# The modulation vector's sixty tiles: from pairs of loads inside the FFN to single loads spread from the merge to the FFN's end

## The chip, the cores and the metric

The kernel runs on one core of a Trainium2 chip. The core has five engines with a queue of instructions each: TensorE (PE, the matmuls, with its weight loads shown apart as PEld), VectorE (DVE), ScalarE (ACT), GpSimd (POOL) and SyncE (SP, which here only issues DMA transfers). Each engine works off its queue in order, and a wait at the head of a queue holds up all that stands behind it. The metric is the time of one execution on the device in microseconds (us); lower is better.

## The reference

Two layers follow each other on 512 tokens of width 1024, in fp32. The first is a hybrid of attention and a state space, with a gated FFN and a per-layer embedding (PLE). The second is a block whose norms and residuals are modulated by a vector computed from a conditioning vector `c_2`:

```python
# first layer, second half
h = h + (gate_attn * attn_d + gate_ssm * ssm_d) @ w_out          # merge, w_out
n2 = rmsnorm(h, g_ffn)
h = h + (silu(n2 @ w_ffn_gate) * (n2 @ w_ffn_up)) @ w_ffn_down   # FFN
h = h + sigmoid(h @ w_ple_gate) * (p_l @ w_ple_proj)             # PLE
...
# second layer
c_act = silu(c_2)
mod = c_act @ w_ada + b_ada                  # [6 * 1024], w_ada is 1024 x 6144
shift1, scale1, gate1, shift2, scale2, gate2 = split(mod, 6)
h = rmsnorm(x, norm1_g) * (1 + scale1) + shift1
proj = h @ w_in
...
```

`mod` depends on the inputs alone, so it can be computed anywhere before the second layer.

## The kernel before, in words

All activations lie feature-major, 128 features by 512 tokens to a tile. A product in fp32 is three matmuls: each operand is split into a high part and a rest (`wh`, `wl` for weights, `..h`, `..l` for activations), and `mm()` issues `wh` by high (L159), `wh` by rest (L160) and `wl` by high (L161). One matmul here has 128 x 128 weights and 512 tokens.

Weights come in tiles of 128 x 1024 fp32 (512 KB). `weights()` allocates a raw tile `wr` (three buffers), issues its load on SP's queue (L150), lets ACT copy the high part to `wh` (L122) and DVE subtract for `wl` (L123); `wh`/`wl` have two buffers. It does so at a priority 40 places ahead of the code around it. The next load into a `wr` buffer is issued when the `wl` that reads it has ended. The order on each engine is set by a scheduler, by priorities in the order of the program.

The stages that the change touches, all in `block_1` (their stretches in the profile in brackets): the gates (to 447.87 us); the **merge** (447.87 to 513.15), 8 turns of 36 matmuls with one `w_glu` tile each and one `w_ap` tile every second turn, after which DVE forms `gb` (L874) and `g` (L873, L875), POOL adds and DVE splits (L129); **w_out** (513.15 to 561.87), 8 turns of 24 matmuls; **gate/up** (561.87 to 813.87), 22 turns of 48 matmuls with one `w_fg` and one `w_fu` tile each; **down** (819.30 to 924.02 without its first stripe), 8 stripes of 66 matmuls with three weight tiles each. Then PLE and the second layer, whose first use of `mod` is at L950.

The modulation vector is the generator `modulation()` (L315). It broadcasts `c_2` over all partitions (L320) and applies Silu (L321) to get `ca`; then, for each of 48 tiles of `w_ada`, it loads 512 KB into `wa` (two buffers, L324) and runs one DVE multiply-and-reduce over 1024 elements (L325), which gives 128 entries of `mod`. Two further tables of 6 tiles each (`w_lat_t`, `w_up_t`) are reduced in the same way (L348, L349) against a row of `mod` that small matmuls (L343) and ACT (L345) broadcast. In all there are 60 loads and 60 reductions. Before, the generator is opened in stage gate/up and advanced twice at the end of each turn of it, and twice in each of the 8 iterations of down as long as anything is left:

```python
for f in range(22):
    ...
    hid.append(self.split_new(hp, f"hid{f}", a))
    for _ in range(2):
        next(mod, None)
```

Of the kernel before, what the change touches and what calls it, by code (L numbers as in the profile page):

```python
# [84 lines left out]
class Program:  # L85
# [53 lines left out]
    def weights(self, ap, n, eng=None, pool=None, bufs=1, parts=1):  # L139

        r = self.t(self.wp, "wr", (128, 8, 128), F32, 3)
        if pool is None:
            h, l = self.pair(self.wp, "w", (128, 8, 128), 2)
        else:
            h, l = self.pair(pool, "ws", (128, n, 128), bufs)
        p0 = self.tc.cur_priority
        self.tc.cur_priority = max(0, p0 - WLEAD[self.phase])
        for i in range(0, n, n // parts):
            b = slice(i, i + n // parts)
            self.Q.dma_start(r[:, b], ap[:, b])  # L150
            self.last_split = self.split(h[:, b], l[:, b], r[:, b], eng)
        self.tc.cur_priority = p0
        return h, l
# [161 lines left out]
    def modulation(self, pool):  # L315
# [6 lines left out]
        for n in range(48):  # L322
            w = self.t(pool, "wa", (128, 1024), bufs=2)
            self.Q.dma_start(w, self.d["w_ada"][n])  # L324
            V.tensor_tensor_reduce(out=w, in0=w, in1=ca, op0=OP.mult, op1=OP.add, scale=1.0, scalar=0.0,  # L325
                                   accum_out=self.mod[:, n:n + 1])
            if n % 8 == 7:
                m = self.mod[:, n - 7:n + 1]
                V.tensor_tensor(out=m, in0=m, in1=self.col("b_ada", n - 7, 8), op=OP.add)
                if n // 8 in (1, 4):  # L330
                    V.tensor_scalar(m, m, 1.0, None, op0=OP.add)
            yield
        self.eb = self.t(self.cp, "eb", (128, len(LAT) + 2 * UPS))
        n = 0
        for m, tab, c in ((0, "w_lat_t", len(LAT)), (3, "w_up_t", 2 * UPS)):
# [10 lines left out]
            for i in range(c):  # L346
                w = self.t(pool, "wa", (128, 1024), bufs=2)
                self.Q.dma_start(w, self.d[tab][i])  # L348
# [3 lines left out]
                yield  # L352

# [406 lines left out]
    def block_1(self):  # L760
# [89 lines left out]
        self.phase = 2  # L850
        m_cm, m = self.open("M")
# [8 lines left out]
        for j in range(8):  # L860
# [16 lines left out]
            self.split_half(merged[j][0], merged[j][1], ga)  # L877
        b_cm.__exit__(None, None, None)
# [8 lines left out]
        for j in range(8):  # L887
# [9 lines left out]
            self.add_square(wo, acc, self.res[j], j == 0)  # L897
        self.y = y
# [7 lines left out]
        mod = self.modulation(hp)  # L906
        hid = []
        for f in range(22):
# [11 lines left out]
            for _ in range(2):  # L920
                next(mod, None)
        self.y = []
        for j in range(8):
# [6 lines left out]
            for _ in range(2):  # L930
# [3 lines left out]
        h_cm.__exit__(None, None, None)  # L934

# [574 lines left out]
```

## Time and profile before

| | before |
|---|---|
| median of 3 runs | 1872.27 us (1864.81 to 1877.15) |
| profiled execution | 1869.56 us |
| its span, first to last instruction | 1867.8 us |
| mean granted clock of TensorE | 0.98 of 2.4 GHz |
| PE busy | 1802.1 us (96%) |
| DVE busy | 1113.7 us (60%) |
| ACT / POOL busy | 42% / 22% |
| DMA in slices 13 to 16 of 40 (560 to 747 us) | 8, 8, 7, 6 tenths; 221, 254, 270, 257 GB/s |
| DMA over the span | mean 110 GB/s |

The profile is one execution. Times of single instructions and waits are read from its trace; engine names with a q (SPq) are an engine's sequencer or its issued transfers. A matmul row shows 0.39 us because matmuls are pipelined: two that follow each other start 0.23 us apart. The granted clock is a share of 2.4 GHz, whose lower level is 1.2 GHz (0.5); a stretch with 0.89 has spent part of its time at the lower level.

### The profile page before, as it was taken

How to read it: one execution, taken by the hardware profiler on the slowest of the kernel's cores; microseconds unless marked ns; L12 is line 12 of the kernel's file. 1: busy time of each engine (PE TensorE's matmuls, PEld its weight loads, DVE VectorE, ACT ScalarE, POOL GpSimd, SP SyncE). 2: the span in 40 equal slices, each digit the busy share in tenths (PEclk: the TensorE clock that was granted, in tenths of full speed). 3: DMA queues.
4: the chain of work that ended last, by engine and by line, in shares of the span. 5: the costliest groups of instructions: out<-in, count | busy, mean ns of one | idle time of the engine just before them, and what ended most of it. 6: DMA issues, size and time to landing. Idle time of an engine off the chain costs nothing.

```text
span 1867.8 us, 22362 instructions
## 1 busy us (share of the span) xinstructions
PE 1802.1 (96%) x8426; PEld 1488.1 (80%) x8426; DVE 1113.7 (60%) x1891; ACT 785.4 (42%) x1189; POOL 405.4 (22%) x277
## 2 busy tenths in 40 slices
PE   8989999999999999999999889999899999999998
PEld 6778888888888777888888767788688788888887
DVE  8866866544556777543355898667633576555323
ACT  4444544343333223322245677658323354444331
POOL 1654412100221111110033544021311211111000
PEclk9988999999999999999999999999999999999999
DMA  6222222242326887333353111132233423333332
GB/s 212 78 73 74 81 87 79 79 135 91 102 91 221 254 270 257 124 95 93 103 172 102 51 35 35 63 101 91 72 102 109 130 90 99 94 101 90 96 100 77
DMA packets 78908, 205.83 MB, mean 110 GB/s; under 512 B 18208, under 2 KB 25120, under 8 KB 78800
## 3 DMA queue, kind: packets, MB, share of 16 engines
q1 hardware_dynamic: 78800, 204.40, 34.7%
q8 instruction: 66, 1.08, 0.3%
q14 instruction: 42, 0.34, 0.1%
HBM read 197.06 MB, written 7.31 MB: 109 GB/s over the span
## 4 chain that ended last, share of the span: by engine, by line
PE 69%; DVE 12%; DMA 8%; issue 4%; ACT 3%; POOL 3%; SPq 1%; POOLq 0%; DVEq 0%; ACTq 0%
PE mm L161 12%; PE mm L159 12%; PE mm L160 12%; DMA wa<-in_w_ada 5%; PE sc L161 5%; PE sc L160 4%; PE sc L159 4%; PE po L161 2%; PE po L159 2%; PE po L160 2%; PE pt L161 2%; PE pt L160 2%; PE pt L159 2%; DVE wa L325 2%; DVE wl L123 2%
## 5 line engine op out<-in xcount | busy, mean ns | idle before, releaser
L122 ACT ACTIVATE wh<-wr 128x1024 fp32r<-128x1024 f32 (+3 forms) x295 | 300.1, 1017 | 579.3 <-PE mm L160 281.6
L123 DVE TENSOR_TENSOR wl<-wr,wh 128x1024 fp32r<-128x1024 f32 (+3 forms) x287 | 354.1, 1234 | 316.3 <-ACT wh L122 305.1
L918 POOL TENSOR_TENSOR fa<-fa,fb 128x512 f32<-128x512 f32 x22 | 40.0, 1818 | 214.2 <-DVE fb L917 187.6
L325 DVE CUSTOM_DVE_ANT_0 wa<-wa,ca 128x1024 f32<-128x1024 f32 x48 | 61.3, 1282 | 31.8 <-DMA wa<-in_w_ada 29.8
L1360 POOL TENSOR_TENSOR f<-f,f 128x512 f32<-128x512 f32 x22 | 29.3, 1334 | 205.6 <-DVE f L1357 168.8
L627 POOL TENSOR_TENSOR tsh<-tsh,sinp 32x512 f32<-32x512 f32 x16 | 41.3, 2584 | 91.0 <-DVE tsh L626 81.7
L202 POOL TENSOR_TENSOR acc<-acc,sq 128x512 f32<-128x512 f32 x28 | 42.3, 1523 | 80.8 <-ACT sq L201 80.8
L161 PE MATMUL mm<-y0h,wl 128*128 128x512 f32 x107 | 45.0, 421 | 7.8 <-DVE wl L123 7.2
L159 PE MATMUL mm<-y0h,wh 128*128 128x512 f32 x107 | 44.0, 411 | 8.2 <-ACT wh L122 6.1
L367 ACT ACTIVATE sm<-sm,st,cols 128x128 f32<-128x128 f32 (+1 forms) x64 | 41.5, 650 | 20.3 <-DVE st L366 16.5
L876 POOL TENSOR_TENSOR g<-g,g 128x512 f32<-128x512 f32 x8 | 17.3, 2166 | 148.8 <-DVE g L875 148.8
L159 PE MATMUL mm<-y1h,wh 128*128 128x512 f32 x107 | 43.5, 407 | 0.2 <-ACT y1h L789 0.2
L160 PE MATMUL mm<-y3l,wh 128*128 128x512 f32 x107 | 42.5, 397 | 1.0 <-DVE y3l L790 1.0
L160 PE MATMUL mm<-y1l,wh 128*128 128x512 f32 x107 | 43.2, 404 | 0.1
L160 PE MATMUL mm<-y4l,wh 128*128 128x512 f32 x107 | 42.6, 398 | 0.6 <-DVE y4l L790 0.6
L160 PE MATMUL mm<-y2l,wh 128*128 128x512 f32 x107 | 43.1, 403 | 0.0
L160 PE MATMUL mm<-y0l,wh 128*128 128x512 f32 x107 | 43.1, 403 | 0.0
L161 PE MATMUL mm<-y1h,wl 128*128 128x512 f32 x107 | 43.0, 402 | 0.0
L159 PE MATMUL mm<-y3h,wh 128*128 128x512 f32 x107 | 42.8, 400 | 0.0
L159 PE MATMUL mm<-y2h,wh 128*128 128x512 f32 x107 | 42.8, 400 | 0.0
L161 PE MATMUL mm<-y2h,wl 128*128 128x512 f32 x107 | 42.7, 399 | 0.0
L159 PE MATMUL mm<-y7h,wh 128*128 128x512 f32 x107 | 42.7, 399 | 0.0
(2180 smaller groups left out, 5599.1 us busy)
## 6 DMA issues: line engine op xcount, KB each, us to landing
wr<-in_w_in SPq DMA_DIRECT2D x86, 512.0 KB, 3.3
wa<-in_w_ada SPq DMA_DIRECT2D x48, 512.0 KB, 4.5
wr<-in_w_up SPq DMA_DIRECT2D x44, 512.0 KB, 3.5
wr<-in_w_fg SPq DMA_DIRECT2D x22, 512.0 KB, 4.4
wr<-in_w_fu SPq DMA_DIRECT2D x22, 512.0 KB, 4.0
wr<-in_w_out SPq DMA_DIRECT2D x16, 512.0 KB, 3.4
wr<-in_w_fd SPq DMA_DIRECT2D x16, 448.0 KB, 3.3
wr<-in_w_down SPq DMA_DIRECT2D x16, 448.0 KB, 3.3
```

What stands on the lines that cost most here:

```text
L122: i = self.S.activation(h, src, AF.Copy)
L123: (eng or self.V).tensor_tensor(out=l, in0=src, in1=h.bitcast(F32), op=OP.subtract)
L159: self.P.matmul(ps, lhsT=ah, rhs=bh, start=first and i == 0, stop=False)
L160: self.P.matmul(ps, lhsT=ah, rhs=bl, start=False, stop=False)
L161: self.last_mm = self.P.matmul(ps, lhsT=al, rhs=bh, start=False, stop=last and i == n - 1)
L202: self.G.tensor_tensor(out=acc, in0=acc, in1=q, op=OP.add)
L325: V.tensor_tensor_reduce(out=w, in0=w, in1=ca, op0=OP.mult, op1=OP.add, scale=1.0, scalar=0.0, accum_out=self.mod[:, n:n + 1])
L367: i = S.activation(sm[:, :w], sm[:, :w], AF.Exp, bias=st[:, 1:2], scale=scale, accum_out=st[:, 2:3])
L627: (V if ROPE_DVE else self.G).tensor_tensor(out=sh, in0=sh, in1=sin, op=OP.mult)
L876: G.tensor_tensor(out=ga, in0=ga, in1=gs, op=OP.add)
L918: G.tensor_tensor(out=a, in0=a, in1=b, op=OP.mult)
L1360: G.tensor_tensor(out=ab[0], in0=ab[0], in1=ab[1], op=OP.mult)
```

## The change

The same tiles are loaded and the same reductions run; their places change, and how a load is placed.

- The generator gets a pool of its own, opened before the merge, and is advanced once per turn of the merge (8), of w_out (8) and of gate/up (22), and three times per iteration of down; that leaves 22 of the 60 tiles for down.
- The load of each `wa` goes through `modulation_tile()`, which places it on SP's queue directly behind the load of the last weights that were issued at that point of the program (`issue_after(self.last_load.ins)`). Lines behind L324 are numbered 5 to 8 higher in the changed file.

```diff
--- before.py
+++ after.py
@@ -147,7 +147,7 @@
         self.tc.cur_priority = max(0, p0 - WLEAD[self.phase])
         for i in range(0, n, n // parts):
             b = slice(i, i + n // parts)
-            self.Q.dma_start(r[:, b], ap[:, b])
+            self.last_load = self.Q.dma_start(r[:, b], ap[:, b])
             self.last_split = self.split(h[:, b], l[:, b], r[:, b], eng)
         self.tc.cur_priority = p0
         return h, l
@@ -320,8 +320,7 @@
         self.Q.dma_start(ca, self.d["c_2"].to_broadcast([128, 1024]))
         self.S.activation(ca, ca, AF.Silu)
         for n in range(48):
-            w = self.t(pool, "wa", (128, 1024), bufs=2)
-            self.Q.dma_start(w, self.d["w_ada"][n])
+            w = self.modulation_tile(pool, self.d["w_ada"][n])
             V.tensor_tensor_reduce(out=w, in0=w, in1=ca, op0=OP.mult, op1=OP.add, scale=1.0, scalar=0.0,
                                    accum_out=self.mod[:, n:n + 1])
             if n % 8 == 7:
@@ -344,12 +343,18 @@
                                   start=True, stop=True)
                 self.S.activation(row[:, 512 * o:512 * o + 512], p, AF.Copy)
             for i in range(c):
-                w = self.t(pool, "wa", (128, 1024), bufs=2)
-                self.Q.dma_start(w, self.d[tab][i])
+                w = self.modulation_tile(pool, self.d[tab][i])
                 V.tensor_tensor_reduce(out=w, in0=w, in1=row, op0=OP.mult, op1=OP.add, scale=1.0, scalar=0.0,
                                        accum_out=self.eb[:, n:n + 1])
                 n += 1
                 yield
+
+    def modulation_tile(self, pool, ap):
+
+        w = self.t(pool, "wa", (128, 1024), bufs=2)
+        with self.tc.issue_after(self.last_load.ins):
+            self.Q.dma_start(w, ap)
+        return w
 
     def mcol(self, m, k):
         return self.mod[:, m * 8 + k:m * 8 + k + 1]
@@ -848,6 +853,8 @@
 
         self.psum(mm=3, sc=2, pt=2, po=1)
         self.phase = 2
+        mod_cm, mp = self.open("mod")
+        mod = self.modulation(mp)
         m_cm, m = self.open("M")
         b_cm, bp = self.open("B")
         merged = [self.pair(m, f"m{j}") for j in range(8)]
@@ -875,6 +882,7 @@
             V.scalar_tensor_tensor(gs, gs, 1.0, gb, op0=OP.add, op1=OP.mult)
             G.tensor_tensor(out=ga, in0=ga, in1=gs, op=OP.add)
             self.split_half(merged[j][0], merged[j][1], ga)
+            next(mod)
         b_cm.__exit__(None, None, None)
         gg_cm.__exit__(None, None, None)
         x1_cm.__exit__(None, None, None)
@@ -895,6 +903,7 @@
             V.scalar_tensor_tensor(l, self.res[j], g, h.bitcast(F32), op0=OP.mult, op1=OP.subtract)
             y.append((h, l))
             self.add_square(wo, acc, self.res[j], j == 0)
+            next(mod)
         self.y = y
         r = self.rsqrt_cols(wo, self.token_sums(acc), NB, "r2", 1.0 / 1024)
         self.spread(self.r1, r)
@@ -903,7 +912,6 @@
 
         self.phase = 3
         h_cm, hp = self.open("H")
-        mod = self.modulation(hp)
         hid = []
         for f in range(22):
             pg = self.ps("mm")
@@ -917,8 +925,7 @@
             V.tensor_tensor(out=b, in0=pu, in1=self.r1, op=OP.mult)
             G.tensor_tensor(out=a, in0=a, in1=b, op=OP.mult)
             hid.append(self.split_new(hp, f"hid{f}", a))
-            for _ in range(2):
-                next(mod, None)
+            next(mod)
         self.y = []
         for j in range(8):
             p = self.ps("mm")
@@ -927,11 +934,12 @@
             h, l = self.pair(self.yp, f"y{j}")
             self.split(h, l, self.res[j])
             self.y.append((h, l))
-            for _ in range(2):
+            for _ in range(3):
                 next(mod, None)
         for _ in mod:
             pass
         h_cm.__exit__(None, None, None)
+        mod_cm.__exit__(None, None, None)
 
         rt_cm, rt = self.open("RC")
         self.rt_cm = rt_cm
```

**SP's queue in gate/up**, where `wr` are weights and `wa` the modulation's tiles. Before, as the modulation starts:

```order
L320 DMA ca<-in_c 128x1024
L324 DMA wa<-in_w_ada 128x1024 x2
L150 DMA wr<-in_w_fu 128x1024
L324 DMA wa<-in_w_ada 128x1024 x2
L150 DMA wr<-in_w_fg 128x1024
```

After, at the passage from w_out to gate/up:

```order
L150 DMA wr<-in_w_out 128x1024
L356 DMA wa<-in_w_ada 128x1024
L150 DMA wr<-in_w_fg 128x1024
L150 DMA wr<-in_w_fu 128x1024
L356 DMA wa<-in_w_ada 128x1024
```

Before, two `wa` stand between any two weights (in places three), until the 60 are through; now one stands behind each `fg`, `fu` pair, and one behind each `w_glu` and each `w_out`. In down the order is now three `w_fd`, two `wa`, the next stripe's first `w_fd`, one `wa`, and so on. `ca` is loaded in the stage of the gates, between two `w_in` loads, and its Silu stands there on ACT with one more table load ahead of it.

**DVE in the merge**, from the split of one turn's result (`m1l`) to the next weights' rest. Before:

```order
L129 SCALAR_TENSOR_TENSOR m1l<-g_3503,m1h 128x512
L874 TENSOR_TENSOR gb<-mm,gb 128x512
L875 SCALAR_TENSOR_TENSOR g_3605<-g_3605,gb 128x512
L123 TENSOR_TENSOR wl<-wr,wh 128x1024
L873 SCALAR_TENSOR_TENSOR g_3639<-g_3639,sc 128x512
```

After, the same turn:

```order
L129 SCALAR_TENSOR_TENSOR m1l<-g_3503,m1h 128x512
L324 ISA wa,mod<-wa,ca 128x1024
L324 ISA mod 128x1
L881 TENSOR_TENSOR gb<-mm,gb 128x512
L882 SCALAR_TENSOR_TENSOR g_3605<-g_3605,gb 128x512
L123 TENSOR_TENSOR wl<-wr,wh 128x1024
L880 SCALAR_TENSOR_TENSOR g_3639<-g_3639,sc 128x512
```

The reduction (two rows, the second reads out the sum) now stands ahead of `gb`, `g` and the next `wl`, in this form or nearly so in the turns of the merge from the second on. 

**DVE at the passage from the merge to w_out**, from the split of the last merged tile (`m7l`) to the first output's rest (`y0l`); `res` is the sum of a finished turn of w_out with the residual. Before:

```order
L129 SCALAR_TENSOR_TENSOR m7l<-g_3911,m7h 128x512
L891 TENSOR_TENSOR res_4463<-mm,res_4463 128x512
L123 TENSOR_TENSOR wl<-wr,wh 128x1024
L891 TENSOR_TENSOR res_4464<-mm,res_4464 128x512
L895 SCALAR_TENSOR_TENSOR y0l<-res_4463,cols,y0h 128x512
```

After:

```order
L129 SCALAR_TENSOR_TENSOR m7l<-g_3911,m7h 128x512
L324 ISA wa,mod<-wa,ca 128x1024
L324 ISA mod 128x1
L899 TENSOR_TENSOR res_4495<-mm,res_4495 128x512
L899 TENSOR_TENSOR res_4496<-mm,res_4496 128x512
L123 TENSOR_TENSOR wl<-wr,wh 128x1024 x2
L903 SCALAR_TENSOR_TENSOR y0l<-res_4495,cols,y0h 128x512
```

Here a reduction has come in, and the `wl` that the third turn of w_out reads stands behind the sums of the first two turns, where before it stood between them.

In gate/up each reduction stands behind both `wl` of its turn. PE's order changes in two ways: the 32 small matmuls of L343 stand partly in gate/up and partly in down, and one group of L190 has moved before two matmuls at the start of gate/up. The loads of the second layer's rotary tables (L266) stand one place earlier in PLE.

## Rows read from the trace of the kernel before

**Rows 1.** The page, part 1 (busy time) and part 4 (chain, by line).

```profile
PE 1802.1 (96%) x8426; PEld 1488.1 (80%) x8426; DVE 1113.7 (60%) x1891; ACT 785.4 (42%) x1189; POOL 405.4 (22%) x277
...
PE mm L161 12%; PE mm L159 12%; PE mm L160 12%; DMA wa<-in_w_ada 5%; PE sc L161 5%; PE sc L160 4%; PE sc L159 4%; PE po L161 2%; PE po L159 2%; PE po L160 2%; PE pt L161 2%; PE pt L160 2%; PE pt L159 2%; DVE wa L325 2%; DVE wl L123 2%
```

**Rows 2.** What PE waited for, 575 to 762 us: total, times, longest.

```profile
PE mm L161 <- DVE wl L123: 5.4, 3, 2.2
PE sc L161 <- DVE wl L123: 3.7, 4, 1.9
```

**Rows 3.** What DVE waited for, same stretch: total, times, longest.

```profile
DVE wa L325 <- DMA wa<-in_w_ada: 29.8, 32, 2.5
```

**Rows 4.** Stretches: us, busy PE, PEld, DVE, ACT, POOL, granted clock, DMA share, GB/s.

```profile
447.87:513.15 65.28, 65.28 (x290) 54.06 (x289) 34.64 (x42) 23.78 (x30) 15.12 (x7) 1.00 0.29 97
513.15:561.87 48.72, 48.57 (x214) 39.90 (x213) 24.71 (x28) 19.10 (x26) 14.48 (x8) 1.00 0.29 96
561.87:813.87 252.00, 242.77 (x1061) 198.24 (x1060) 169.24 (x235) 73.84 (x92) 38.84 (x22) 0.98 0.66 214
561.87:575.31 13.44, 13.44 (x68) 11.36 (x67) 3.31 (x5) 2.75 (x4) 1.02 (x1) 1.00 0.33 112
...
597.07:608.43 11.36, 11.36 (x53) 9.46 (x52) 9.27 (x14) 3.28 (x4) 2.14 (x2) 1.00 0.78 255
608.43:624.37 15.94, 13.71 (x57) 11.12 (x56) 10.62 (x16) 3.61 (x5) 2.57 (x2) 0.89 0.80 255
...
660.62:675.31 14.69, 12.90 (x50) 9.99 (x49) 10.45 (x16) 3.83 (x6) 3.65 (x2) 0.88 0.82 276
675.31:719.50 44.19, 44.10 (x196) 36.02 (x194) 34.88 (x54) 13.56 (x18) 7.61 (x4) 1.00 0.84 274
...
759.47:813.87 54.40, 54.40 (x242) 45.05 (x241) 27.14 (x26) 16.90 (x22) 7.31 (x5) 1.00 0.30 99
819.30:924.02 104.72, 104.72 (x463) 86.72 (x462) 33.01 (x35) 25.22 (x29) 2.19 (x1) 1.00 0.33 96
```

**Rows 5.** Line L343 over the whole span: count, shortest/median/longest ns.

```profile
L343 PE MATMUL pt<-ident,mod x32: 270/275/276, 603.0 to 736.2; 128*128 128x128 f32 x32
```

**Rows 6.** Timeline of DVE, 614 to 618 us.

```profile
615.22 1.23 DVE L325 CUSTOM_DVE_ANT_0 wa<-wa,ca 128x1024 f32<-128x1024 f32 x1 [1.77 <-DMA wa<-in_w_ada]
...
616.37 1.22 DVE L123 TENSOR_TENSOR wl<-wr,wh 128x1024 fp32r<-128x1024 f32 x1
```

**Rows 7.** Timeline of PE, 614 to 650 us; in brackets the idle time before.

```profile
617.64 0.72 PE L161 MATMUL mm<-y0h,wl 128*128 128x512 f32 x1 [2.23 <-DVE wl L123]
...
619.01 0.63 PE L161 MATMUL mm<-y1h,wl 128*128 128x512 f32 x1
...
649.75 0.50 PE L161 MATMUL sc<-y0h,wl 128*128 128x512 f32 x1 [0.62 <-DVE wl L123]
```

**Rows 8.** Timeline of one turn of the merge, 464 to 468 us.

```profile
464.46 0.69 DVE L874 TENSOR_TENSOR gb<-mm,gb 128x512 f32<-128x512 f32 x1 [2.77 <-PE mm L161]
...
465.79 1.22 DVE L123 TENSOR_TENSOR wl<-wr,wh 128x1024 fp32r<-128x1024 f32 x1
...
467.04 0.33 SPq L150 DMA_DIRECT2D wr<-in_w_glu  x1
...
467.81 0.39 PE L161 MATMUL sc<-yss0h,wl 128*128 128x512 f32 x1
```

**Rows 9.** DMA issues, 571.2 to 572.3 us: count, KB, us from issue to landing.

```profile
wr<-in_w_fg SPq DMA_DIRECT2D x1, 512.0 KB, 3.2
ca<-in_c SPq DMA_DIRECT2D x1, 512.0 KB, 5.2
wa<-in_w_ada SPq DMA_DIRECT2D x1, 512.0 KB, 6.0
```

**Rows 10.** Timeline of SP's queue, the same three issues.

```profile
571.27 0.33 SPq L150 DMA_DIRECT2D wr<-in_w_fg  x1
...
572.12 0.90 SPq L324 DMA_DIRECT2D wa<-in_w_ada  x2
```

## The prediction

> **What bounds the kernel now.** I read the page first. PE is busy 96% of the span and fills most of the chain of waits; beside it the chain holds two things that belong to the modulation vector, 5% for the loads of its tiles and 2% for their reductions, and 2% for the weights' rest `wl` [rows 1]. So the kernel is bound by PE nearly everywhere, and the modulation shows on the chain in one stage. The windows say which: in gate/up PE is busy 242.77 of 252.00 us and the clock is 0.98, while DMA runs at 214 GB/s, against 96 to 99 in the merge, in w_out, in down and in the last five turns of gate/up, where PE has no idle worth naming [rows 4]. There the price of an undisturbed turn can be read: 54.40 / 5 = 10.88 us.
>
> The waits in the stretch with the 60 loads tell how the loads reach PE. PE waited 5.4 + 3.7 = 9.1 us, always for `wl` on DVE [rows 2], and DVE itself waited 29.8 us in 32 places for a tile of `w_ada` [rows 3]. One place shows both: DVE sat 1.77 us until a tile had landed, reduced it, and only then came to the `wl` that stood behind it [rows 6]; PE had been idle for 2.23 us by then, and its next matmuls last 0.63 us where 0.39 is usual [rows 7, 8]. That window has a granted clock of 0.89: a part of it ran at 1.2 instead of 2.4 GHz. An idle of 0.62 us elsewhere was not followed by such a fall [rows 7]. The DMA engines are not the limit by themselves: in 675 to 719 us they moved 274 GB/s and PE lost 0.09 of 44.19 us [rows 4].
>
> **What the change removes.** The 21 turns of gate/up (one of the 22 lies across the edges) would take 21 x 10.88 = 228.5 us; they take 252.00, so 23.5 are lost. Of these, the first window loses 13.44 - 10.88 = 2.56 at the start of the FFN (token sums and their spread), which no load of the modulation causes. The small matmuls of L343 cost (11.36 - 10.88) / 4 = 0.12 us each, by the window that holds four of them and no wait, and there are 32: 3.8 us [rows 4, 5]. They stay, if elsewhere. What is left, 23.5 - 2.56 - 3.8 = **17.1 us**, is idle PE (9.1) and what follows it at the lower clock or in restarting (8.0). For example, the window from 660.62 us is 14.69 - 10.88 = 3.81 too long: 14.69 - 12.90 = 1.79 of it idle, and 2.0 at the lower clock (0.88 granted) [rows 4].
>
> Does all of it go? In gate/up there is one load to two weights now, and its reduction stands behind both `wl` of its turn, about one half turn (5.44 us) after the point from which its load could start. Should it come late all the same, a `wl` behind it still has 5.44 - 1.22 for itself [rows 6] and about as much for `wh` on ACT, so some 3 us, before PE wants it. The traffic is 99 GB/s plus 22 x 0.524 MB / 239 us = 48, so 147 against 274 carried without idle. I take 0 loss; the floor is 0, since no less can be lost, and the cost if the cover failed is one idle as in [rows 7]. In down 22 tiles bring 96 + 22 x 0.524 / 104.72 us = 206 GB/s, and DVE 33.01 + 22 x 1.23 = 60 of 104.72 us [rows 4]; the third load of a stripe waits for a buffer, but its reduction stands behind the sum of the stripe that ends, so late. I take 0, with up to 2 for the entry into down, where three reductions stand in a row.
>
> **What it adds in the merge.** Here a ring closes that was not there. Before, DVE is idle 2.77 us ahead of `gb`, and from the start of `gb` to the end of `wl` it takes 465.79 + 1.22 - 464.46 = 2.55 us; SP issues the next weights 0.03 us after that `wl`, and PE wants `wl` at 467.81, 0.80 us after its end [rows 8]. Now a tile of the modulation is issued behind those weights, and its reduction stands ahead of the next `gb` on DVE, so of `g`, of the next `wl`, and by the freed buffer of the next weights' load. From `wl` to `wl` this takes 0.03 + L + 1.15 (a reduction, from 615.22 to 616.37 in [rows 6]) + 2.55 = 3.73 + L, where L is the time from the issue of the weights to the landing of the tile behind them. A turn of PE takes 65.28 / 8 = 8.16 us, so the ring costs nothing up to **L = 4.4**.
>
> L has to come from the one burst in the trace: weights, `ca` and a tile issued 0.43 us apart landed 3.2, 0.43 + 5.2 = 5.6 and 0.85 + 6.0 = 6.85 us after the first issue [rows 9, 10]. From one load to the next that is 2.4 and 1.2 us; so a pair lands at 3.2 + 1.2 = 4.4 at the best, at 5.6 at the worst, and I take the mean of the two steps, L = 5.0. A turn is then 8.73 us, 0.57 too long. There are 7 hand-overs from turn to turn, the slack of 0.80 goes first, and in one turn `wl` stands ahead of `g` and saves 0.6: 7 x 0.57 - 0.8 - 0.6 = **+2.6 us**, with 0 at L = 4.4 and 7 x 1.17 - 1.4 = 6.8 at L = 5.6.
>
> The Trainium skill, on its page "DMA: Bandwidth & Descriptors", section "Anatomy of one DMA — SWDGE (gpsimd) path", fits a transfer as some 2.0 us plus its bytes at 436 GB/s. For one tile that gives an estimate of 3.2 us, as the burst's first row has it; for the pair it gives 4.4, and then the ring just closes and the merge loses nothing. For all three it would give 5.6, where the trace has 6.85, and that speaks against it here.
>
> At the passage to w_out the lag of the last turn delays `g`, POOL's sum and `m7`, for which w_out's first two turns keep their last matmuls; and the `wl` of the third turn now stands behind the sum of the second. From that turn's end to that `wl` DVE needs 0.69 + 1.22 = 1.9 us, of which PE covers four matmuls (0.9). I take 1.0 for each of the two: **+2.0**, from 1 to 3.
>
> **Without a price.** `ca`, its Silu (one pass over 1024 elements) and one table load more stand on ACT in the gates' stage; ACT is busy 42% [rows 1]; the loads of the rotary tables stand one place earlier in PLE. In w_out DVE has 24.71 of 48.72 us [rows 4] and gets 8 reductions, 9.8. All of these I take at 0, within 1 either way.
>
> **The sum.** 1869.56 - 17.1 + 2.6 + 2.0 = 1857.1 for an execution like the profiled one. That lies 2.7 below the median of the three runs, so against the median it is 1872.27 - 12.5 = 1859.8: I predict **1860**.
>
> **Rivals.** (A) The forecast, L between 4.6 and 5.6: 1857 to 1865. (B) No ring: the pair lands by 4.4, and only the passage costs something: 1872.3 - 17.1 + 0 to 2 = 1855 to 1857. For it speaks the step of 1.2 us between the burst's last two rows; against it the step of 2.4 before. (C) The change buys little: the ring runs at L = 5.6 to 6.3 because the rest of the weights' load is in its way, 6.8 to 12 us, with 3 at the passage, or some of the 17.1 stays in gate/up: 1862 to 1870. (D) Slower than before: in the merge a pair takes as long as the third transfer of the burst, L = 6.85. The ring is then 10.58 us, 2.42 above PE's turn, and seven of them cost 15.5 after the slack; an idle of that length is one after which [rows 7] shows the lower clock, which adds up to 2.0 each where the ring does not hide it. With 3 at the passage that is 18.5 to 32.5, against 17.1 won: 1874 to 1888. It decides from L = 6.6, or earlier if the clock falls. Against it: that row had two transfers ahead of it, not one, and the merge's other traffic is only 97 GB/s.
>
> **How the numbers follow.** A 0.56, B 0.20, C 0.14, D 0.08, and 0.02 for what I have not thought of. The predicted time is A's. The three runs of before differ by 0.7%, so a median may lie some 4 us off; the range 1850 to 1870 holds A and B with that margin and nearly all of C, and leaves out D. A change of 1% (19 us) is about what a measurement of this kernel can tell from none. A gain of more than that (below 1853.5) needs B with a favourable median, or that 1 or 2 us come from the places I took at 0: 0.16. Slower by over 1% (above 1891) is the far end of D: 0.05. The rest, 0.79, is within 1%.
>
> **What would show it.** In gate/up PE's waits for `wl` should vanish and its clock be 1.00, the stage some 17 to 19 us shorter. In the merge, PE should wait for `wl` about 0.6 us in five or six turns with the clock at 1.00, and DVE should wait there for `wa` ahead of each reduction; the stretch should be 67 to 69 us long instead of 65.28. A tile behind one weight should land some 4.6 us after its own issue. Down should have no wait of PE. The prediction is wrong if the merge is not longer at all (B), if its turns pass 9.5 us (C, D), or if waits for `wl` are left in gate/up or appear in down.

## The result

The changed kernel takes 1854.68 us (median of 11 runs, 1846.41 to 1858.62) against 1869.14 us (median of 11 runs of the kernel before, 1861.79 to 1877.15; the three runs of the table above are among them). The ratio is 0.9928, 95% interval 0.9912 to 0.9944, so the change gives 13.5 us, 10.5 to 16.4. The forecast was 1860, a gain of 12.5.

The page of the profile after, part 1 and the chain by line, as in [rows 1]:

```profile
PE 1792.1 (97%) x8426; PEld 1481.2 (80%) x8426; DVE 1133.5 (61%) x1891; ACT 787.4 (43%) x1190; POOL 394.0 (21%) x277
...
PE mm L159 14%; PE mm L161 14%; PE mm L160 14%; PE sc L161 5%; PE sc L160 5%; PE sc L159 5%; PE po L161 2%; PE po L160 2%; PE po L159 2%; PE pt L161 2%; PE pt L160 2%; PE pt L159 2%; DMA wa<-in_w_ada 2%; DVE wl L123 2%; POOL tsh L632 1%
```

The modulation's loads have gone from 5% of the chain to 2%, and its reductions from 2% to below the last entry shown. What PE waited for between 440 and 930 us, that is from the merge to down:

```profile
PE sc L161 <- DVE wl L123: 1.9, 5, 1.2
PE mm L159 <- ACT wh L122: 0.7, 2, 0.5
```

All of it lies in the merge and at its end. In gate/up, where [rows 2] has 9.1 us, PE waits for nothing. DVE's wait for tiles of `w_ada` in gate/up (29.8 us in 32 places in [rows 3]):

```profile
DVE wa L324 <- DMA wa<-in_w_ada: 1.9, 2, 1.2
```

The stretches: merge, w_out, gate/up, the second and third turn of it, its other turns, down without its last stripe (the stretch of 819.30 to 924.02 us before, too, holds the first seven of the eight stripes). The columns are those of [rows 4]:

```profile
444.47:514.12 69.65, 67.51 (x289) 53.56 (x288) 45.55 (x59) 23.78 (x30) 14.21 (x7) 1.00 0.44 155
514.12:563.85 49.73, 49.05 (x215) 39.77 (x213) 36.60 (x47) 19.46 (x26) 14.14 (x8) 1.00 0.49 172
563.85:796.78 232.93, 232.93 (x1045) 193.44 (x1043) 138.19 (x149) 70.94 (x87) 28.99 (x22) 1.00 0.40 139
578.19:600.94 22.75, 22.75 (x105) 18.94 (x104) 12.85 (x14) 6.58 (x9) 2.59 (x2) 1.00 0.34 118
600.94:796.78 195.84, 195.84 (x866) 162.25 (x864) 119.13 (x126) 59.10 (x73) 24.09 (x18) 1.00 0.42 143
802.22:908.83 106.61, 106.61 (x480) 88.56 (x478) 57.62 (x80) 27.31 (x33) 1.98 (x1) 1.00 0.60 197
```

Against [rows 4]: the merge takes 4.37 us more, w_out 1.01 more, gate/up 19.07 less, down 1.89 more; from the first turn of the merge to the last stripe of down 476.15 has become 464.36, **11.8 us less**. The granted clock is 1.00 throughout, where gate/up had 0.98, and 18 turns run at 195.84 / 18 = 10.88 us, the undisturbed price. The span fell by 18.7 (1867.8 to 1849.1); the other 6.9 lie ahead of the merge, which began 3.4 us earlier, and behind down. Nothing shows that they are the change's: in the profiles of the kernels below the merge begins anywhere from 442.8 to 453.2 us, and in that of run 11, the changed kernel again, at 448.26.

The chain in the merge. It is the ring: tile, reduction, `gb`, `g`, `wl`, the next load on SP, and the next tile (start, duration, what):

```profile
474.14 6.26 DMA wa<-in_w_ada
...
483.80 4.53 DMA wa<-in_w_ada
...
488.35 0.04 DVE wa L324
488.38 1.12 issue
489.50 0.08 DVE mod L324
489.58 0.61 DVE gb L881
...
490.26 0.57 issue
490.83 1.23 DVE wl L123
...
492.08 0.33 SPq L150
```

From the issue of a tile at 483.80 us to its landing it takes 4.53 us, and from `wl` to `wl` some 8.6 us. One tile took 6.26 us. On SP's queue a weights' load of `w_ap` follows it after 1.9 us, but one follows the tile of two turns earlier after as long:

```profile
456.92 0.43 SPq L356 DMA_DIRECT2D wa<-in_w_ada  x1
458.78 0.33 SPq L150 DMA_DIRECT2D wr<-in_w_ap  x1
...
474.14 0.43 SPq L356 DMA_DIRECT2D wa<-in_w_ada  x1
476.00 0.33 SPq L150 DMA_DIRECT2D wr<-in_w_ap  x1
```

The DMA view of the two turns, from 456.5 to 464 us and from 473.7 to 482 us (queue: packets, MB, share; issues with the time to landing):

```profile
q1 hardware_dynamic: 432, 1.57, 58.0%
...
wa<-in_w_ada SPq DMA_DIRECT2D x1, 512.0 KB, 4.5
```

```profile
q1 hardware_dynamic: 432, 1.57, 53.3%
q8 instruction: 1, 0.02, 0.7%
...
wa<-in_w_ada SPq DMA_DIRECT2D x1, 512.0 KB, 6.3
```

The same loads stand in both; only the slow turn has a packet of 16 KB on the queue that the profile names "instruction". In runs 3 and 11, whose order is that of the changed kernel, the tile of this turn took 6.39 and 6.12 us, again with one such packet. Over all profiles, from 380 to 1000 us, of the tiles issued 0.38 us behind a weight with nothing else in flight and no further load within 1.5 us, 140 without such a packet landed after 4.2 to 4.8 us, 14 of them with another load 1.5 to 3 us behind; of 39 with one, 20 took 5.3 to 7.3 us. No run takes the packets away, so that they cause the delay is not shown.

The DMA issues from 447 to 505 us, with the time from issue to landing:

```profile
wa<-in_w_ada SPq DMA_DIRECT2D x8, 512.0 KB, 4.6
wr<-in_w_glu SPq DMA_DIRECT2D x6, 512.0 KB, 3.6
```

### The profile page after: what moved, and what is told of

It reads as the page before. It is cut to its first block, busy times and chain, and to the rows that moved or that the text cites. A ratio compares the mean times of both kernels' runs of the same rounds, so it can differ in the third digit from the quotient of the medians.

```text
span 1849.1 us, 22289 instructions
## 1 busy us (share of the span) xinstructions
PE 1792.1 (97%) x8426; PEld 1481.2 (80%) x8426; DVE 1133.5 (61%) x1891; ACT 787.4 (43%) x1190; POOL 394.0 (21%) x277
## 4 chain that ended last, share of the span: by engine, by line
PE 76%; DVE 11%; issue 4%; POOL 3%; DMA 3%; ACT 2%; SPq 0%; POOLq 0%; DVEq 0%; ACTq 0%
PE mm L159 14%; PE mm L161 14%; PE mm L160 14%; PE sc L161 5%; PE sc L160 5%; PE sc L159 5%; PE po L161 2%; PE po L160 2%; PE po L159 2%; PE pt L161 2%; PE pt L160 2%; PE pt L159 2%; DMA wa<-in_w_ada 2%; DVE wl L123 2%; POOL tsh L632 1%
## 5 line engine op out<-in xcount | busy, mean ns | idle before, releaser
L123 DVE TENSOR_TENSOR wl<-wr,wh 128x1024 fp32r<-128x1024 f32 (+3 forms) x287 | 371.3, 1294 | 294.0 <-ACT wh L122 281.9
L324 DVE CUSTOM_DVE_ANT_0 wa<-wa,ca 128x1024 f32<-128x1024 f32 x48 | 62.6, 1303 | 30.9 <-DMA wa<-in_w_ada 30.7
L926 POOL TENSOR_TENSOR fa<-fa,fb 128x512 f32<-128x512 f32 x22 | 29.9, 1361 | 209.3 <-DVE fb L925 194.1
L925 DVE TENSOR_TENSOR fb<-sc,r 128x512 f32<-128x512 f32 x22 | 15.2, 691 | 67.1 <-PE sc L161 67.1
L883 POOL TENSOR_TENSOR g<-g,g 128x512 f32<-128x512 f32 x8 | 16.4, 2052 | 156.2 <-PE sc L161 121.0
L161 PE MATMUL mm<-y7h,wl 128*128 128x512 f32 x107 | 42.5, 397 | 0.0
```

What stands on the lines that cost most here:

```text
L123: (eng or self.V).tensor_tensor(out=l, in0=src, in1=h.bitcast(F32), op=OP.subtract)
L161: self.last_mm = self.P.matmul(ps, lhsT=al, rhs=bh, start=False, stop=last and i == n - 1)
L883: G.tensor_tensor(out=ga, in0=ga, in1=gs, op=OP.add)
L926: G.tensor_tensor(out=a, in0=a, in1=b, op=OP.mult)
```

## The experiments

The stretch from the merge's first turn to the last stripe of down is the one that the change touches; its length in each run's profile stands beside the times, since times differ by several us with what lies outside it. Its **floor** follows from undisturbed rows: merge 65.28, w_out 48.72, gate/up 228.48 + 2.56, 5.44 for its last half turn ahead of down, down 104.72, and L343's 3.84, in all 459.04 us. The kernel before takes 476.15 there, the changed one 464.36.

**1. Spreading without placement** (`e1`). The changed kernel, its tiles' loads left to the scheduler.

```diff
-        with self.tc.issue_after(self.last_load.ins):
-            self.Q.dma_start(w, ap)
+        self.Q.dma_start(w, ap)
```

> The change without its placement: the modulation is opened before the merge and advanced as in the changed kernel, but each load stands where the scheduler puts it. It puts about a dozen of the 60 loads into the gates' stage and 29 into the merge, two to four between any two weights. Theory (placement is what counts; a weight or a split of weights behind a tile that is still on its way costs PE): 29 tiles of 0.524 MB and the merge's own 6.3 MB are 21.5 MB, at 274 GB/s 79 us instead of 65.3, so the merge loses 13 or more and gate/up gains about 17: 1860 to 1875. Rival (it is the place in the program alone, spreading the tiles over more stages, that helped): gate/up has its 17 us and nothing is lost elsewhere, 1852 to 1857.

Measured: 1871.28 us, ratio 1.0026 (1.0009 to 1.0043); the stretch 473.86 us. The windows show the merge, two of its turns, and gate/up:

```profile
451.40:531.10 79.70, 69.68 (x290) 54.54 (x288) 66.26 (x97) 23.55 (x29) 11.53 (x7) 0.98 0.75 245
460.20:472.91 12.71, 10.24 (x37) 7.93 (x38) 11.24 (x15) 2.71 (x5) 2.06 (x1) 0.87 0.73 222
482.30:492.87 10.57, 8.46 (x38) 6.68 (x37) 8.78 (x11) 3.39 (x5) 2.14 (x1) 1.00 0.69 222
580.14:815.10 234.96, 234.96 (x1061) 195.24 (x1059) 124.47 (x130) 73.19 (x91) 30.64 (x22) 1.00 0.36 118
```

The merge is 14.4 us longer at 245 GB/s, gate/up is as fast as it can be. The gain is not the spreading's: it only moves the stalls to where the tiles go. Whether it is the order on DVE or the traffic that costs PE there, this run can't tell.

**2. Placement without spreading** (`e2`). The kernel before with `modulation_tile()` alone; opened in gate/up, two steps per turn, as before.

```diff
-            w = self.t(pool, "wa", (128, 1024), bufs=2)
-            self.Q.dma_start(w, self.d["w_ada"][n])
+            w = self.modulation_tile(pool, self.d["w_ada"][n])
```

> The placement without the spreading: the modulation is opened in gate/up as before and advanced twice per turn there and twice per iteration of down, but each load stands behind the last weights issued. From the sixth turn on SP's queue has fg, fu and two tiles, and both reductions stand together behind the second wl of a turn; the first five turns are still interleaved. Theory (placement counts): the stalls of gate/up go except for 1 to 4 us in the first turns, the merge is as before (no ring), so 1852 to 1857, within 3 us of the changed kernel. Rival (the rate counts, one tile to two weights is what the stage can carry): two tiles per turn still hold up a wl, at least half of the 17 us stays, 1861 or more.

Measured: 1848.17 us, ratio 0.9900 (0.9880 to 0.9920); the stretch 459.11 us. Merge and gate/up:

```profile
448.42:513.70 65.28, 65.28 (x290) 54.05 (x288) 34.63 (x42) 23.79 (x30) 15.11 (x7) 1.00 0.29 97
562.42:795.44 233.02, 233.02 (x1045) 193.36 (x1043) 159.71 (x202) 73.69 (x88) 31.48 (x22) 1.00 0.56 195
```

It beats the expectation of the theory: the first, still interleaved turns cost nothing. (That tells little, as in the kernel before, too, PE's first wait in gate/up comes only at 617.64 us [rows 7].) Two tiles per turn are no load that the stage can't carry; the merge's ring is not needed for anything. But two per turn are fewer than before. There the generator is advanced twice per turn, yet the scheduler ran about four reductions per turn, two ahead of each `wl`, and was through early; here and in run 6 they are two per turn. The 48 reductions of `w_ada` in the kernel before (within 137 us, some 12 turns) and in run 6 (within 245 us); shortest/median/longest ns, first and last start:

```profile
L325 DVE CUSTOM_DVE_ANT_0 wa<-wa,ca x48: 1210/1226/2285, 579.3 to 715.9; 128x1024 f32<-128x1024 f32 x48
...
L327 DVE CUSTOM_DVE_ANT_0 wa<-wa,ca x48: 1209/1212/2312, 578.5 to 823.2; 128x1024 f32<-128x1024 f32 x48
```

So the placement also halves the rate, and this run doesn't separate the two.

**3. Reduction one step later** (`e3`). The changed kernel, `yield` between a tile's load and its reduction.

```diff
             w = self.modulation_tile(pool, self.d["w_ada"][n])
+            yield
             V.tensor_tensor_reduce(out=w, in0=w, in1=ca, ...
...
-            yield
```

> The changed kernel with each reduction one step later than its load: a step reduces the tile that the step before has loaded, then issues the next load. In the merge the reduction stands in the same place of DVE's queue, but its tile has had a turn to land. Theory (the merge's 4.4 us are a ring through the load's time to land): the merge falls from 69.65 to 65.3 to 65.8 us and the passage to w_out loses 0.5 or less, 4 to 5 us less in all, 1849 to 1851. Rival (they are DVE's own time, a reduction of 1.23 us ahead of gb, g and wl): the merge stays above 68.5, 1853 to 1856.

Measured: 1851.51 us, ratio 0.9921 (0.9903 to 0.9939); the stretch 463.72 us. The merge:

```profile
449.10:518.10 69.00, 66.79 (x289) 53.65 (x288) 45.36 (x59) 23.74 (x30) 14.22 (x7) 1.00 0.43 156
```

The theory's figure was missed, but the run tells nothing between the two: the order came out as in the changed kernel on every engine, but for one small DVE instruction that changes its place in run 11, too. So this is the changed kernel a second time. Why the scheduler put the reductions back is not shown. In the chain the tile's load still stood ahead of each reduction. Run 5 does what this one meant to.

**4. Without the merge** (`e4`). The changed kernel, started in w_out, four steps per iteration of down.

```diff
-            next(mod)             # in the merge
...
-            for _ in range(3):
+            for _ in range(4):
```

> The changed kernel without the merge: the modulation starts in w_out, and down takes four tiles per iteration instead of three. Theory: the merge is as before, 65.3 us, and since in w_out and gate/up nothing else changes, 4 to 5 us go, less what four tiles per stripe cost in down (1.43 MB of weights and 2.1 MB of tiles in 14.96 us are 236 GB/s, below the 274 that were carried without idle): 1849 to 1852. Rival (down is where the tiles hold up weights next, since SP now has tiles between the parts of a stripe's weights): PE waits for wl in down by 0.5 us or more per stripe and loses its clock there, 1855 to 1865.

Measured: 1849.27 us, ratio 0.9912 (0.9896 to 0.9929); the stretch 459.35 us. Merge and down:

```profile
449.25:514.63 65.38, 65.38 (x289) 53.98 (x288) 38.12 (x46) 23.79 (x30) 15.12 (x7) 1.00 0.35 118
801.95:908.60 106.65, 106.65 (x479) 88.51 (x478) 67.47 (x96) 27.07 (x33) 1.98 (x1) 1.00 0.69 237
```

As the theory had it. Down carries 237 GB/s without idle PE; its 1.9 us above 104.72 are L343's 16 matmuls there.

**5. The changed kernel with the reductions behind `wl`** (`e5`). `last_wl` is the DVE instruction that `weights()` issued last.

```diff
-            V.tensor_tensor_reduce(out=w, in0=w, in1=ca, ...
+            with self.tc.issue_after(self.last_wl.ins):
+                V.tensor_tensor_reduce(out=w, in0=w, in1=ca, ...
```

> The changed kernel with one edge more: each reduction is queued on DVE behind the wl of the weights behind whose load its tile is queued, so that in the merge it stands behind a wl and ahead of the next g, and no longer ahead of gb and the next wl. The reduction of a turn is then wanted some 8 us after its load was issued, and the tile needs 4.9. Theory (the merge's 4.4 us are the ring wl, weights' load, tile's load, reduction, gb, g, wl): the merge returns to 65.3 us with the same loads and the same 1.23 us per reduction on DVE, the passage to w_out to 48.7 to 49.3, so 1848 to 1850. Rival (DVE's added 1.23 us per turn or the added traffic of 64 GB/s slow the merge): it stays above 68 us, 1853 to 1856.

Measured: 1851.95 us, ratio 0.9914 (0.9889 to 0.9938); the stretch 459.22 us. The merge, and what DVE waited for in it:

```profile
450.26:515.54 65.28, 65.28 (x290) 54.07 (x288) 50.72 (x61) 23.79 (x30) 15.12 (x7) 1.00 0.46 153
```

```profile
DVE gb L884 <- PE mm L162: 13.9, 7, 4.3
DVE g L850 <- PE mm L162: 3.3, 1, 3.3
DVE wl L123 <- ACT wh L122: 0.2, 1, 0.2
```

As many loads and reductions stand in the merge, give or take one, DVE is busier than in the changed kernel, and the 4.4 us are gone; DVE waits for no tile. So they were the ring, and neither DVE's time nor the traffic: here the place alone has changed, at the same rate. The time itself is above what was expected by 2 us, which the stretch doesn't show.

**6. The kernel before with the same edge alone** (`e6`). The edit is that of run 5, on the kernel before; no load is placed.

> The kernel before, with that edge alone: reductions queued behind the last wl of their point of the program, loads of the tiles left to the scheduler, two per turn as before. On SP's queue two tiles then stand between fg and the next fu in every turn, since a buffer comes free only with its reduction. Theory (PE lost its 17 us to a wl that stood on DVE behind a reduction whose tile was still on its way; where the loads stand on SP's queue counts only through that): the stalls go, within 2 us of the run with placed loads, 1847 to 1851. Rival (weights that queue on SP behind two tiles come late themselves): PE waits for wh or wl in gate/up, at least 6 us stay, 1855 or more.

Measured: 1850.95 us, ratio 0.9911 (0.9883 to 0.9940); the stretch 459.07 us. Gate/up, and DVE's wait for tiles there:

```profile
561.15:794.19 233.04, 233.04 (x1045) 193.39 (x1044) 161.44 (x200) 73.83 (x88) 30.67 (x22) 1.00 0.58 195
```

```profile
DVE wa L327 <- DMA wa<-in_w_ada: 2.9, 4, 1.4
```

PE waits nowhere between 440 and 930 us. One edge on DVE gives what the change gives, and what the ring costs on top. With the edge a buffer comes free only behind a `wl`, and two tiles between `fg` and `fu` on SP's queue do no harm, so at two tiles per turn the place on SP's queue is not what counts. Like run 2, this run has two reductions per turn where the kernel before had about four (DVE has 200 instructions in gate/up, 235 before). A run with four per turn, all behind both `wl`, was not made: how much of the 17 us is the reductions' place and how much their rate stays open.

**7. Reductions without loads** (`e7`). The kernel before; all reductions read one resident tile.

```diff
-            w = self.t(pool, "wa", (128, 1024), bufs=2)
-            self.Q.dma_start(w, self.d["w_ada"][n])
-            V.tensor_tensor_reduce(out=w, in0=w, in1=ca, ...
+            w = self.t(pool, "wa", (128, 1024), bufs=2)
+            V.tensor_tensor_reduce(out=w, in0=wk, in1=ca, ...
```

> The kernel before with all 60 reductions but one load: every reduction reads the same resident tile of w_ada, so mod and all that follows from it have other values; 59 loads of 0.5 MB are left out. The reductions now run in a dense row on DVE early in gate/up, up to three between two wl. Theory (the price was the wait for tiles on their way): DVE's 60 times 1.23 us alone cost PE nothing or nearly so, gate/up is 233 to 236 us, 1848 to 1853. Rival (DVE's time was the price): gate/up keeps idle PE ahead of wl, half of the 17 us or more, 1858 or more.

Measured: 1855.27 us, ratio 0.9935 (0.9906 to 0.9964); the stretch 465.50 us. Gate/up:

```profile
560.87:802.21 241.34, 237.83 (x1061) 194.17 (x1059) 178.71 (x235) 74.12 (x92) 38.14 (x22) 1.00 0.28 95
```

Neither theory nor rival. With no tile to wait for, gate/up still takes 241.34 where all of L343 in it would leave 228.48 + 2.56 + 3.84 = 234.88: 6.5 us, from reductions that mostly stand three or four between two `wl`. In the kernel before they are mostly two, and three in five places, so this is DVE's time in a denser order than it had there. It is not free where it is piled up in front of what PE waits for.

**8. Two tiles per turn in the merge** (`e8`).

```diff
-            next(mod)             # in the merge
+            for _ in range(2):
+                next(mod)
...
-            for _ in range(3):    # in down
+            for _ in range(2):
```

> The changed kernel with two tiles per turn of the merge instead of one, two per iteration of down instead of three. It loads the ring: behind each glu weight stand two tiles, and one or both reductions stand ahead of the next wl. By the ring's sum with the second tile landing some 1.2 to 1.4 us after the first, L = 6.1 to 6.3, and one reduction more: turns of 9 to 10 us, the merge 72 to 79 us, 3 to 9 above the changed kernel's, at full clock: 1857 to 1863. The slow rival of the prediction (idle of 1.8 us or more per turn brings the lower clock, and it adds): turns of 11 us or more, the merge above 82, 1867 or more.

Measured: 1852.90 us, ratio 0.9932 (0.9905 to 0.9960); the stretch 463.86 us. The merge and two of its turns:

```profile
444.17:514.08 69.91, 66.58 (x289) 53.74 (x288) 54.08 (x75) 23.45 (x29) 10.74 (x7) 1.00 0.56 200
452.33:462.42 10.09, 8.49 (x37) 6.68 (x36) 7.72 (x10) 3.35 (x5) 2.06 (x1) 1.00 0.40 141
471.95:480.11 8.16, 8.16 (x37) 6.76 (x36) 7.84 (x10) 3.22 (x4) 1.30 (x1) 1.00 0.53 189
```

The merge is as long as with one tile per turn, below what was expected, because the order was not the one assumed in each turn. In the four turns in which both reductions stand ahead of a `wl` it takes 8.78 to 10.09 us; where the scheduler put the `wl` between them, 8.16. Each at a clock of 1.00, so there is no sign of the slow rival.

**9. Spreading with the edge on DVE** (`e9`). Run 1 with the edit of run 5.

> The run with spreading alone, which lost 14.4 us in the merge, with the edge on DVE: reductions queued behind the wl of their point of the program, loads of the tiles left to the scheduler. A buffer now comes free only behind a wl, so the loads spread by themselves, one to a weight. Theory (what counts is that no wl stands on DVE behind a reduction whose tile is on its way; an order on SP's queue is not needed): merge 65.3 and gate/up 233 us with no wait of PE above 0.5, the stretch from the merge to the last stripe of down 459 to 460 us, 1848 to 1852. Rival (the placement on SP's queue is needed once the tiles are spread over the merge): the merge stays above 67.5 us, 1854 or more.

Measured: 1850.74 us, ratio 0.9909 (0.9895 to 0.9924); the stretch 459.27 us. Merge and gate/up:

```profile
451.67:516.95 65.28, 65.28 (x289) 54.08 (x288) 50.72 (x61) 23.78 (x30) 15.12 (x7) 1.00 0.48 154
565.94:798.87 232.93, 232.93 (x1044) 193.44 (x1043) 139.66 (x151) 70.95 (x87) 28.98 (x22) 1.00 0.44 141
```

The theory's figures. The run that lost 14.4 us in the merge loses nothing once no `wl` stands behind a tile on its way; the placement on SP's queue isn't needed. The edge also thinned the merge out, from 25 reductions to 9 and from 245 to 154 GB/s. Traffic of that size alone cost PE nothing in down in run 4 (237 GB/s) and 0.09 of 44.19 us in [rows 4] (274), but place and rate are not separated here either.

**10. Waits without DVE's time** (`e10`). The kernel before, reductions over 64 elements.

```diff
-            V.tensor_tensor_reduce(out=w, in0=w, in1=ca, ...
+            V.tensor_tensor_reduce(out=w[:, :64], in0=w[:, :64], in1=ca[:, :64], ...
```

> The kernel before with all 60 loads and reductions over the first 64 of 1024 elements only (the rest of the sum is left out, so mod has other values): a reduction takes about 0.15 us instead of 1.23, its wait for the tile stays. The order on SP and DVE is nearly that of before. With the run without loads, where 8.3 us were left of gate/up's 17 with DVE's time alone, this gives the other part. Theory (waits and DVE's time add in front of a wl): what the waits alone cost is the rest, 6 to 12 us, gate/up 239 to 245 us. Rival 1 (the waits alone cost nearly all, since a shorter reduction only means a longer wait for the next tile): 246 us or more. Rival 2 (waits alone are covered by the 3 us that a wl has in hand, only with DVE's time do they reach PE): below 237 us.

Measured: 1852.75 us, ratio 0.9929 (0.9908 to 0.9950); the stretch 462.49 us. Gate/up, and DVE's wait for tiles of `w_ada` in it:

```profile
556.81:795.14 238.33, 235.86 (x1060) 195.17 (x1059) 112.49 (x235) 74.14 (x92) 37.34 (x22) 1.00 0.69 226
```

```profile
DVE wa L325 <- DMA wa<-in_w_ada: 61.1, 43, 3.0
```

The 8.3 us in the expectation were wrongly counted for run 7, against a gate/up from which half of L343 had gone; by the same floor they are 6.5. Here 238.33 - 234.88 = 3.4 us are left, although DVE waited twice as long for tiles as before. The 238.33 us lie in the gap between the two, 0.7 below what the theory allowed and 1.3 above the second rival's bound: waits alone are mostly, but not wholly, covered by what a `wl` has in hand. Runs 7 and 10 together make 6.5 + 3.4 = 9.9 of the 17.1 us. That is no clean split, since the reductions of run 7 stand denser and the waits of run 10 are longer than in the kernel before. But most of what is missing has a name. In gate/up of the kernel before the clock fell three times, each time for a stretch like this one, at a granted 0.50:

```profile
617.75:621.16 3.41, 3.41 (x9) 2.64 (x10) 2.26 (x5) 0.00 (x0) 0.00 (x0) 0.50 0.92 255
```

The three together are 10.2 us, which at 1.00 would take half: 5.1 us. Runs 7 and 10 have 1.00 throughout, with single waits of PE of 1.1 and 1.5 us at the longest, where those before the three falls were 2.2, 1.8 and 1.9. Idle PE is 9.23 us before, 3.51 in run 7 and 2.47 here.

**11 and 12. The changed kernel beside one with both edges, on one chip** (`e11`, `e12`). The second is run 2 with the edit of run 5; its order turned out the same as that of run 6 on every engine.

> The changed kernel itself, on the same chip as the next run, so that the ring and the passage (4.4 and 1.0 us by the profile) can be told from noise in the times: ratio to before 0.9925 to 0.9940, 4 to 6 us above the next run.

> The modulation in gate/up as before, two tiles per turn, with both edges: loads behind the last weights' load, reductions behind the last wl. The order is nearly that of the run with the edge on DVE alone. Theory: the stretch from the merge to the last stripe of down stands at its floor, 459.0 to 459.2 us, PE never waits in it, 4 to 6 us below the changed kernel. Rival (the differences among the runs that take 459 to 464 us there are lost in the noise of the rest): no difference beyond the intervals.

Measured: the changed kernel 1855.04 us, ratio 0.9947 (0.9930 to 0.9964), stretch 463.60; both edges 1850.34 us, ratio 0.9921 (0.9896 to 0.9947), stretch 459.07. The changed kernel's merge and the other's gate/up:

```profile
448.26:517.15 68.89, 66.82 (x289) 53.65 (x288) 45.30 (x59) 23.78 (x30) 14.25 (x7) 1.00 0.43 157
```

```profile
567.16:800.20 233.04, 233.04 (x1045) 193.34 (x1043) 161.12 (x200) 73.82 (x88) 30.67 (x22) 1.00 0.58 195
```

The medians lie 4.7 us apart, as far as expected, and the stretches 4.5, while the changed kernel's ratio came out above what was expected and the two intervals overlap a little. With run 3 the changed kernel's order was measured three times, at 0.9921, 0.9928 and 0.9947, and the first is the ratio of the kernel with both edges: the times don't tell the two apart for certain. The stretch does, by one profile each: 463.60 to 464.36 us in the three, 459.07 to 459.35 in the five programs that differ in where the loads stand (runs 2, 4, 5, 6 and 9, ratios 0.9900 to 0.9914). Run 2 or run 6 is the version to keep.

## Why the prediction was right

**What goes in gate/up** was 17.1 us. Gate/up fell by 19.07, of which 1.9 are 16 of the 32 small matmuls of L343 that now stand in down, where they reappear as 1.89: 17.2 us. The working assumed that all of the loss hung on a `wl` behind tiles on their way. That it came to PE through the `wl` on DVE is shown: PE waited for nothing else [rows 2], and in run 6 an edge on DVE alone brings it back in full. That the reductions' own time takes part in it (run 7) was not in the working, and neither was that the change lowers the rate, from about four reductions per turn to one. How the 17 us divide between place and rate stays open (runs 2 and 6).

**The ring in the merge** was 2.6 us, from 0 to 6.8, and is 4.4 in the profile after and 3.6 in run 11. The mechanism holds in each part (the chain after; run 5). L was taken as 5.0; 483.80 + 4.53 less the weights' issue 0.38 earlier is 4.91, and most turns take 8.58 to 8.69 us, where the sum had 8.73. With L = 4.9 the sum would have given 7 x 0.47 - 1.4 = 1.9. What it had no term for are tiles that are late: in the profile after, the first took 5.47 us, about 1.0 too long, and that of the fourth hand-over 6.26, about 1.75, and both have a packet on the instruction queue beside them. In run 11 one did, 6.12, about 1.6. Taken off, they leave 4.4 - 2.7 = 1.7 and 3.6 - 1.6 = 2.0 us by an estimate, so the ring itself was priced well. PE's waits were not 0.6 us in each turn: they are 1.9 us in all, 1.2 of them in one place, and the other half of the 4.4 us lies in the rows at each hand-over, where the last matmul ahead of a wait counts with its whole 0.39 us and the first behind it lasts 0.50.

The burst was not the only place of the trace to read L from: at 1239.89 us two weights' loads of 512 KB, issued 0.60 us apart with nothing behind them, land 3.5 and 4.1 us after their own issues, so the second 4.70 after the first issue. Of the two steps of the burst, 2.4 and 1.2, the first is that of `ca`, a broadcast. That the mean of the two gave an L near 4.9 was luck.

The Trainium skill ("DMA: Bandwidth & Descriptors", section "Anatomy of one DMA — SWDGE (gpsimd) path") has a fit for transfers issued from GpSimd, which for the bytes of the pair gives an estimate of 4.4. Here 4.9 was measured, so the trace does not agree, and the ring that the fit would have closed without loss did cost; but these loads are issued on SP's queue, so it only shows that the fit does not carry over to them.

**The passage to w_out** was 2.0, from 1 to 3, and is 1.0. PE waited 0.47 and 0.21 us there, and for `wh` on ACT, not for `wl`: `m7` came late, so turn 0 of w_out kept its last matmuls and with them its `wh`/`wl` buffer until turn 1 was nearly done, and ACT could write the third turn's `wh` only then. The half of the term for `m7` had its size; the half for a `wl` behind a sum on DVE did not show, since `wh` was later still.

**Terms at nothing**: down takes 106.61 us, less 16 x 0.12 for L343 104.7, as before; the gates, ACT's Silu and PLE show no difference that stands out from what the executions differ by, which is several us.

**The sum** of the terms was 12.5 us; the stretch shows 11.8, the times 13.5 (10.5 to 16.4). It came out so near in part by luck: the ring cost 1.8 more than its term and the passage 1.0 less. The absolute time came out 5 us below the forecast, mostly since the median of before over 11 runs is 1869.1 and not 1872.3.

**The signs.** Gate/up behaved as foretold: no wait, a clock of 1.00, 19.07 us shorter. The merge did not in full: 69.65 us lie above the 67 to 69 that were named (68.89 in run 11), and one turn, 9.68, passed the 9.5 us that were to speak for C or D; it is the turn of the late tile.

**The rivals**: B (no ring) fell by the chain and run 5, and not by the time, as 1854.68 us lies beside its 1855 to 1857 and below A's 1857 to 1865; C and D fell by the 8.6 us of the other turns. D's price was argued from idle time that would bring the lower clock. That step wasn't sound, as run 1 shows: an idle of 2.5 us was followed by it, one of 2.1 was not (below). The chance of 0.05 for a time above 1891 us was called the far end of D, but D as priced ends at 1888.

## What to carry to other kernels

Look at what stands in an engine's queue ahead of the instruction that the critical engine waits for. A side task whose input is still on its way belongs behind that instruction, and once it stands there it hardly matters how its loads are spread or queued, at the one or two tiles per turn that were tried; here one edge on DVE was worth as much as the re-planned loads, and by the stretch 4.5 to 5.3 us more. Count, too, how many of its steps the scheduler really runs per turn, and not only how often the program advances it. When a side task is placed by its loads instead, check whether load, use and the next load close a ring through a buffer, and compare its sum with the turn it has to fit in.

## What was not expected of the hardware

- The same matmuls, idle for about the same time, did and did not drop to the lower clock. In run 1 the turn from 460.20 us had PE idle for 2.5 us and a granted clock of 0.87, the turn from 482.30 had 2.1 us and 1.00; in the kernel before the clock fell after 1.8 us [rows 4]. In these rows the length of an idle alone does not tell it.
- Two causes in front of a `wl`, a wait and DVE's own time, cost 3.4 and 6.5 us in runs that have one of them and 17.1 in the kernel that has both. The orders differ, so this is no exact sum, but about 5 us of the difference are the lower clock, to which only the kernel with both fell.
- A pair of loads 0.38 us apart lands its second tile after 4.2 to 4.8 us, whether or not another load follows 1.9 us behind. The tiles that took 5.3 to 7.3 us all had a packet of the instruction queue beside them; not every such packet goes with a late tile (the one issued at 501.07 us in the profile after took 4.58).
